# Padding the constant tiles of a two-layer decoder so that the transposed activations begin at a multiple of 64 bytes

## The chip, the cores and the metric

The kernel runs on one core of a Trainium2 chip. The time is device microseconds of that core for one execution. Before the change the median of three runs is 966.6 us (965.89 to 967.51).

## What is computed

A decoder trunk of two layers on 256 tokens of width 1024, in float32. Each layer has three sub-layers with a norm before and after: a SwiGLU (width 2816), a mixer, and a second SwiGLU. Cut to what matters:

```python
for l in range(DEPTH):                                   # DEPTH = 2
    f = swiglu(rms_norm(x, ffn1_pre_g[l]), ffn1_w_gu[l], ffn1_w_down[l])
    x = x + 0.5 * rms_norm(f, ffn1_post_g[l])
    m = hybrid_mixer(rms_norm(x, mix_pre_g[l]), mix_w_in[l], mix_w_out[l], ...)
    x = x + rms_norm(m, mix_post_g[l])
    f = swiglu(rms_norm(x, ffn2_pre_g[l]), ffn2_w_gu[l], ffn2_w_down[l])
    x = x + 0.5 * rms_norm(f, ffn2_post_g[l])

def swiglu(x, w_gu, w_down):
    g, u = jnp.split(x @ w_gu, 2, axis=-1)
    return (jax.nn.silu(g) * u) @ w_down
```

The mixer is one product into 2566 columns, three mixers side by side on groups of those columns (a gated linear recurrence, a state-space scan over two chunks of 128 tokens, and a gated causal mixing over tokens), and one product back to 1024 columns.

## The kernel before

**Numbers.** Every large product is done as three matmuls on values split into a high and a low part: high by high, high by low, low by high. The parts have the type fp32r. Small products (transposes by an identity matrix, the scan's products) are plain fp32.

**The tile nT.** `nT` holds x transposed, 128 features on the partitions, and in each partition `[2, 8, 256]` numbers: the part (high, low), the block of 128 features, and the token. It is written before each sub-layer by `pre` (four transposes into a PSUM bank, a cast for the high part, a subtraction for the low one) and read by two kinds of matmul:

- *A-steps* (line 425, `mm3` called from `a_step`): a 128-token slice of nT is the stationary operand, that is, loaded as weights; the split weights of the model move, 512 or 390 columns. They make the first block of each SwiGLU and the first two groups of the mixer.
- *B-tiles* (line 704, `b_tile`): a 128-column slice of the model's weights is stationary, and 256 tokens of nT move. They make the rest of both SwiGLUs' first products and of the mixer's.

```python
st = tuple(self.nT[:, i, k, t * P:(t + 1) * P] for i in range(2))            # a_step
self.mm3(bk[0][:, :w], st, (wt[:, 0, :w], wt[:, 1, :w]), start, stop)
...
wh, wl = (w[:, i, col:col + P] for i in range(2))                            # b_tile
xh, xl = self.nT[:, 0, k, :], self.nT[:, 1, k, :]
for i, (a, b) in enumerate(((wh, xh), (wh, xl), (wl, xh))):
    self.keep(self.nc.tensor.matmul(out, a, b, start=..., stop=...))
```

The products back to width 1024 (`down`) also go through `mm3` at line 425, but with the hidden values as the stationary operand (slots s_a or s_m) and 512 columns of weights moving. Every such matmul is preceded by one weight load (LDWEIGHTS) of 128 columns.

**Memory of a partition.** Tiles are taken in the order in which they are first asked for, each rounded up to 32 bytes. `setup` takes x0, x1, `pf` (per-feature parameters, 180 numbers, 720 bytes), nT, `ident` (the identity), `tri` (a triangle of ones), `ones` (one number), `ident_r`, `later` and `mhalf` (one number); `layer_params` takes `pb` (530 numbers), `wst`, `wbd` and more. Behind them stand small tiles, three staging buffers `stg` for the weights that come in by DMA, and the slots: `s_w` (17 split weights of 4 KB), `s_a` (13), `s_m` (8), `s_f` (3). The places in bytes of a partition, with the rest that they leave when divided by 64:

| tile | before | rest | after | rest |
|---|---|---|---|---|
| x0, x1, pf | 16512, 20608, 24704 | 0 | the same | 0 |
| nT | 25440 | 32 | 25472 | 0 |
| ident, tri | 41824, 42336 | 32 | 41856, 42368 | 0 |
| ones | 42848 | 32 | 42880 | 0 |
| ident_r, later | 42880, 43392 | 0 | 42944, 43456 | 0 |
| mhalf | 43904 | 0 | 42884 | 4 |
| pb | 43936 | 32 | 43968 | 0 |
| wst, wbd, gp | 46080, 48128, 51200 | 0 | 46144, 48192, 51264 | 0 |
| stg (first), s_a0, s_w0 | 58176, 82752, 90944 | 0 | 58240, 82816, 91008 | 0 |

All slices of nT that matmuls read begin a multiple of 512 bytes behind nT's own start, and so do the slices of the slots that the large products read, so a tile's rest holds for each of its operands there.

**Order.** The order of the work is fixed when the program is built, by a planner with costs of its own (class `Chain`, `pump`, the table `T`); those costs know nothing of addresses. Weights come through the SP queue into `stg`, ScalarE makes the high part (lines 396, 400), VectorE the low part (lines 397, 401), and TensorE uses a slot until `release`.

Of the kernel before, what the change touches and what calls it, by code (L numbers as in the profile page):

```python
# [8 lines left out]
F32 = mybir.dt.float32  # L9
# [6 lines left out]
P = 128  # L16
# [3 lines left out]
DEPTH = 2  # L20
# [84 lines left out]
NP_ = _off  # L105
BCOL = {"dtb": (0, 6), "alog": (6, 6), "dsk": (12, 6), "lng": (18, 256), "lnb": (274, 256)}
NB_ = 530


class Chain:  # L110
    """A side computation: a generator whose operations are issued when their inputs are due."""

    def __init__(self, k, t=None):
        self.k = k
# [107 lines left out]
class Kernel:  # L222
# [35 lines left out]
        self.wt, self.wh, self.wready, self.slot_time = {}, {}, {}, {}  # L258
        self.extra, self.keep_free = 0, 4

    # ---------------------------------------------------------------- memory
    def get(self, shape, dtype=F32, kind="a"):
        tag = self.free_slots[kind].pop(0)
        return self.scr.tile(shape, dtype, tag=tag, name="s_" + tag), (kind, tag)
# [24 lines left out]
        o, w = BCOL[name]  # L289
        return self.pb[:, o:o + w]  # L290

    # ---------------------------------------------------------------- issue order
    def keep(self, ins, pin=False):
        if pin or self.now() < PIN:
            self.tc.keep_in_program_order(ins)
# [39 lines left out]
    def drain(self):  # L335
        self.wait_for(lambda: not self.chains)

    # ---------------------------------------------------------------- weights
    def dma_chunk(self):
        ci = self.next_dma  # L340
        self.next_dma += 1
# [74 lines left out]
        self.slot_time[h] = self.now()  # L416
        self.put(h)

    # ---------------------------------------------------------------- main products
    def mm3(self, out, st, mv, start, stop):  # L420
        (sh, sl), (mh, ml) = st, mv
        mm = self.nc.tensor.matmul
# [11 lines left out]
        st = tuple(self.nT[:, i, k, t * P:(t + 1) * P] for i in range(2))  # L434
        self.mm3(bk[0][:, :w], st, (wt[:, 0, :w], wt[:, 1, :w]), start, stop)

    # ---------------------------------------------------------------- setup
    def setup(self):
        nc, cp = self.nc, self.cp
        self.cur = 0  # L440
        self.x = [cp.tile([P, D], F32, name=f"x{t}") for t in range(2)]
        nc.sync.dma_start(out=self.x[0], in_=self.x_d[0, 0:P, :])
        self.pf = cp.tile([P, DEPTH * NP_], F32, name="pf")
        nc.scalar.dma_start(out=self.pf, in_=self.pf_d)
        self.T["dma"] = 3.4
        self.dma_chunk()
        nc.sync.dma_start(out=self.x[1], in_=self.x_d[0, P:2 * P, :])
        self.T["dma"] += 1.46
        self.nT = cp.tile([P, 2, KT, SEQ], F32R, name="nT")
        self.ident = cp.tile([P, P], F32, name="ident")  # L450
        make_identity(nc, self.ident)
        self.tri = cp.tile([P, P], F32, name="tri")
        make_upper_triangular(nc, self.tri)
        self.ones = cp.tile([P, 1], F32, name="ones")
        nc.gpsimd.memset(self.ones, 1.0)
        self.ident_r = cp.tile([P, P], F32R, name="ident_r")
        nc.scalar.copy(self.ident_r, self.ident)
        self.later = cp.tile([P, P], F32R, name="later")
        nc.vector.tensor_scalar(out=self.later, in0=self.tri, scalar1=1.0, scalar2=1e30, op0=ALU.subtract, op1=ALU.mult)
        self.mhalf = cp.tile([P, 1], F32, name="mhalf")  # L460
        nc.gpsimd.memset(self.mhalf, -0.5)
        self.T["pool"] = 2.0

    def softplus(self, c, out, x, n, tag):
        """out = softplus(x) for [P, n] operands."""
        m, z, z2, p = (self.single([P, n], tag + s) for s in ("m", "z", "q", "p"))
        yield from c.stt(n, m, x, -1.0, x, ALU.mult, ALU.min)
        yield from c.act(n, m, m, AF.Exp, table="exp")
        yield from c.ts(n, z, m, 2.0, ALU.add)
        yield from c.op("dve", 0.15, self.nc.vector.reciprocal, z, z)  # L470
        yield from c.tt(n, z, m, z, ALU.mult)
        yield from c.tt(n, z2, z, z, ALU.mult)
        yield from c.ts(n, p, z2, 1.0 / 15, ALU.mult)
        for k in (13, 11, 9, 7, 5, 3):
            yield from c.stt(n, p, p, 1.0 / k, z2, ALU.add, ALU.mult)
        yield from c.stt(n, p, p, 1.0, z, ALU.add, ALU.mult)
        yield from c.ts(n, m, x, 0.0, ALU.max)
        yield from c.stt(n, out, p, 2.0, m, ALU.mult, ALU.add)

    def layer_params(self, l):  # L480
        nc, lp = self.nc, self.lp
        yield self.now() + 20.0
        self.pb = lp.tile([P, NB_], F32, tag="pb", name="pb")
        self.keep(nc.scalar.dma_start(out=self.pb, in_=self.pb_d[l:l + 1, :].partition_broadcast(P)), True)
        self.wst = lp.tile([P, 4, P], F32, tag="wst", name="wst")
        self.keep(nc.scalar.dma_start(out=self.wst, in_=self.wst_d[l]), True)
        raw, hr = self.get([P, 6, 64], F32, "f")
        self.keep(nc.scalar.dma_start(out=raw, in_=self.wri_d[l]), True)
        self.wbd = lp.tile([P, 6, P], F32, tag="wbd", name="wbd")
        c = Chain(self)  # L490
        c.pin = True
        yield from c.op("pool", 0.8, nc.gpsimd.memset, self.wbd, 0.0)
        c.t += 20.0
        cpy = nc.gpsimd.tensor_copy
        yield from c.op("pool", 0.8, cpy, out=self.wbd[0:64, :, 0:64], in_=raw[0:64])
        yield from c.op("pool", 0.8, cpy, out=self.wbd[64:128, :, 64:128], in_=raw[64:128])
        self.put(hr)
        yield from c.ptt(512, self.wst, self.wst, self.tri.unsqueeze(1).to_broadcast([P, 4, P]), ALU.mult)
        nl = self.single([P, 3], "nl")
        yield from c.ts(3, nl, self.pcol(l, "lam", 0, 3), -1.0, ALU.mult)  # L500
        self.cl = lp.tile([P, 2, 3], F32, tag="cl", name="cl")
        sp = self.single([P, 3], "spl")
        yield from self.softplus(c, sp, nl, 3, "sl")
        yield from c.ts(3, self.cl[:, 0, :], sp, -8.0, ALU.mult)
        yield from c.ts(3, self.cl[:, 1, :], sp, 8.0, ALU.mult)
        self.na = lp.tile([P, 6], F32, tag="na", name="na")
        yield from c.act(6, self.na, self.bcol("alog"), AF.Exp, table="exp")
        yield from c.ts(6, self.na, self.na, -1.0, ALU.mult)
        c.flag(("params", l))
# [3 lines left out]
        self.keep(self.nc.scalar.dma_start(out=t, in_=self.gp_d[i:i + 1, :].partition_broadcast(P)), True)  # L513
        return t

    # ---------------------------------------------------------------- norms
    def rstd_of(self, c, ss, n, eps, name):
        v = self.small(1, name + "v")
        if n == 2:
# [11 lines left out]
        yield from c.act(n, self.junk()[:, :n], src, AF.Square, scale=scale, accum_out=out)  # L531

    def post(self, t, banks, gp, half, nxt):
        """x[t] += (0.5 if half else 1) * rms_norm(result, gp); then the next sub-layer's operand."""
        c = Chain(self)
        ev = self.ev[t]
        ss = self.small(2, "pss")
# [1 line left out]
        for n in range(2):  # L539
            yield from c.until(("acc", self.phase_of(nxt), t, n))  # L540
            a, v = c.fork(), c.fork()
            ps, tag, _ = banks[n]
# [24 lines left out]
        return self.cur_phase  # L567

    def pre(self, t, nxt, halves):
        """The operand of the next sub-layer, x transposed and split into two parts, and 1 / rms(x) by token.  # L570

        Products take x as it is; 1 / rms(x) goes to their results. A swiglu keeps it off u, and with it off
        the whole sub-layer's result, whose own norm then adds eps / rs^2 instead of eps.
        """
        kind, _, ph = nxt
        xt = self.x[t]
        for q in range(2):
            c = halves[q]
            ps, tag = yield from c.aux()
# [8 lines left out]
        c = halves[1]  # L588
# [14 lines left out]
        ps, tag = yield from c.aux()  # L603
# [2 lines left out]
        c.free_aux(tag)  # L606
        c.flag(("rb", ph, t))

    # ---------------------------------------------------------------- ffn
    def evac_block(self, b, g, u, gtag, utag, t, width, hT, ph):  # L610
        c = Chain(self)
        sil, h1 = yield from c.get([P, 512], F32, "m")
# [77 lines left out]
        return self.down(lhs, d, gp, True, nxt)  # L690

    def b_tile(self, bk, half, d, col, last):
        """One 128-column tile of the product, features by tokens."""
        self.T["pe"] = max(self.T["pe"], bk[2] + HOP)
        for t in range(2):
            for q in range(2):
                self.need(("nT", self.phase, t, q))
        out = bk[0][:, half * SEQ:(half + 1) * SEQ]
        for k in range(KT):
            w = self.unit(d + k)  # L700
            wh, wl = (w[:, i, col:col + P] for i in range(2))
            xh, xl = self.nT[:, 0, k, :], self.nT[:, 1, k, :]
            for i, (a, b) in enumerate(((wh, xh), (wh, xl), (wl, xh))):
                self.keep(self.nc.tensor.matmul(out, a, b, start=k == 0 and i == 0, stop=k == KT - 1 and i == 2))  # L704
                self.T["pe"] += SEQ * 0.000417
                self.pump()
            if last:
                self.release(d + k)
# [63 lines left out]
            self.put(*lhs[i][3])  # L772
        return d + 2 * n_k

    # ---------------------------------------------------------------- mixer
    def mixer(self, l, d, nxt):
        nc, ph = self.nc, self.phase
        gp = self.load_gpost(l * 3 + 1)
# [184 lines left out]
            c.flag(("mixT", ph, f, t))  # L963

    def decay(self, l):
        """dt, the decays within a chunk, exp(a_cs[l] - a_cs[s]) for s <= l, and the decays to its ends."""
        nc, M, ph = self.nc, self.M, self.phase
        c = Chain(self)
        d12 = lambda a: a.rearrange("p c h -> p (c h)")
        dt, ad, nacs = (self.single([P, 2, 6], n) for n in ("dt", "ad", "nacs"))  # L970
# [90 lines left out]
        self.put(h_xdt, h_xd, M["zs_h"], M["bc_h"])  # L1061

    def scores(self, c, ch, bT, cT):
        """E[s, l] * (c[l] . b[s]) for s <= l, each head."""
        M, ph = self.M, self.phase
        e = M["E"][ch][0]
        ps, tag = yield from c.aux()
# [46 lines left out]
            yield from self.split_out(c, 3 + f, ch, ps[:, f * P:(f + 1) * P])  # L1114
        c.free_aux(tag)

    # ---------------------------------------------------------------- program
    def build(self):
        self.rs, self.ev = [None, None], [None, None]
        self.setup()  # L1120
# [78 lines left out]
```

## Time and profile before

| what | value |
|---|---|
| median of three runs | 966.6 us |
| profiled execution, first to last instruction | 963.5 us (3.1 us below the median; what lies outside the span is not in the trace) |
| granted TensorE clock | 0.998 of full speed |
| TensorE matmul (PE) | busy 98% of the span |
| weight loads (PEld) | 90%, beside the matmuls |
| VectorE, ScalarE, GpSimd | 67%, 60%, 4% |
| DMA | 182 GB/s in the mean |

A matmul's own duration in the trace is longer than the distance to the next one, since matmuls are pipelined: a 128x256 B-tile matmul is shown as 279 ns long, while they start about 117 ns apart. What one costs is therefore read from the distance between starts: the start of a run of equal matmuls, the start of what follows it, and the count.

### The profile page before, as it was taken

Reading aid. Unit: us, or ns where it says so; the run is one execution under the profiler, and the core shown is the slowest. Engines: PE = TensorE matmul, PEld = TensorE weight load, DVE = VectorE, ACT = ScalarE, POOL = GpSimd, SP = SyncE. Lnnn points to the kernel's source line nnn. Section 1 sums busy time; section 2 is a strip of 40 time slices with the busy share of each in tenths; the row PEclk is TensorE's granted clock in tenths of the full one; section 3 lists DMA queues with packets and bytes.
Section 4 is the critical chain, followed back from the end, with each engine's and each line's share of the span. In section 5 each row is a group of like instructions: output and inputs, shape, how many; then the busy total and the mean of one; then the engine's idle time right before and its main releaser. Section 6 shows DMA issues by size and latency. Waiting matters only on the chain.

```text
span 963.5 us, 16052 instructions
## 1 busy us (share of the span) xinstructions
PE 945.1 (98%) x6292; PEld 862.9 (90%) x6292; DVE 649.1 (67%) x1169; ACT 580.4 (60%) x1057; POOL 40.1 (4%) x58
## 2 busy tenths in 40 slices
PE   7999999999999999999999999999999999999997
PEld 6999998889986999998889999888999779999885
DVE  5876666566899856676565666666588996566632
ACT  7865555576967765555564555555589685454531
POOL 1100000001001100000010000000010110000000
PEclk9999999999999999999999999999999999999999
DMA  8855555443246945566435555663431566455621
GB/s 309 290 202 205 188 208 208 154 168 116 88 136 212 327 165 175 176 218 221 172 130 198 175 183 209 221 224 113 177 127 45 206 231 236 137 193 210 214 80 44
DMA packets 26717, 175.66 MB, mean 182 GB/s; under 512 B 2960, under 2 KB 3344, under 8 KB 7824
## 3 DMA queue, kind: packets, MB, share of 16 engines
q1 hardware_dynamic: 24768, 169.93, 50.0%
q10 hardware_dynamic: 1872, 4.70, 1.4%
q8 instruction: 49, 0.80, 0.3%
q14 instruction: 28, 0.23, 0.1%
HBM read 173.57 MB, written 1.05 MB: 181 GB/s over the span
## 4 chain that ended last, share of the span: by engine, by line
PE 89%; DVE 6%; ACT 2%; POOL 1%; issue 1%; DMA 0%; DVEq 0%; POOLq 0%; ACTq 0%
PE acc L704 46%; PE acc L425 39%; PE acc L137 4%; DVE s_w L401 2%; DVE s_a L137 1%; ACT s_a L137 1%; DVE x L137 1%; DVE s_f L137 1%; POOL postr L137 1%; DVE nT L137 1%; ACT L137 1%; POOL rs L137 0%; DMA x<-in_x_dram 0%; ACT junk L137 0%; POOL lnr L137 0%
## 5 line engine op out<-in xcount | busy, mean ns | idle before, releaser
L704 PE MATMUL acc<-nT,s_w 128*128 128x256 f32 x3900 | 467.5, 279 | 0.0
L704 PEld LDWEIGHTS acc<-nT,s_w 128*128 128x128 f32 x3900 | 460.3, 188 | 0.7
L401 DVE SCALAR_TENSOR_TENSOR s_w<-stg,pf,s_w 128x512 fp32r<-128x512 f32 (+2 forms) x435 | 299.2, 735 | 112.8 <-ACT s_w L400 112.5
L400 ACT ACTIVATE s_w<-stg,pf 128x512 fp32r<-128x512 f32 (+2 forms) x435 | 279.4, 701 | 113.7 <-PE acc L704 62.1
L425 PE MATMUL acc<-s_w,s_a 128*128 128x512 f32 x984 | 227.4, 390 | 0.0
L425 PEld LDWEIGHTS acc<-s_w,s_a 128*128 128x128 f32 x984 | 184.1, 188 | 37.9
L397 DVE TENSOR_TENSOR s_w<-stg,s_w 128x512 fp32r<-128x512 f32 x184 | 121.9, 687 | 61.9 <-ACT s_w L396 61.7
L396 ACT CAST s_w<-stg 128x512 fp32r<-128x512 f32 x184 | 107.0, 619 | 68.6 <-PE acc L425 36.7
L425 PE MATMUL acc<-s_w,nT 128*128 128x512 f32 (+1 forms) x522 | 129.3, 394 | 1.2 <-DVE nT L137 1.0
L425 PEld LDWEIGHTS acc<-s_w,nT 128*128 128x128 f32 x522 | 95.7, 189 | 21.6 <-DVE nT L137 2.3
L137 ACT ACTIVATE s_m<-s_m 128x512 f32<-128x512 f32 x36 | 22.6, 632 | 79.9 <-DVE s_m L137 79.9
L137 DVE TENSOR_TENSOR s_m<-acc,s_m 128x512 f32<-128x512 f32 (+1 forms) x64 | 35.7, 562 | 31.3 <-PE acc L704 25.8
L425 PE MATMUL acc<-s_w,s_m 128*128 128x512 f32 x192 | 48.0, 399 | 0.0
L425 PEld LDWEIGHTS acc<-s_w,s_m 128*128 128x128 f32 x192 | 34.8, 188 | 7.0 <-ACT s_m L137 0.5
L137 POOL TENSOR_TENSOR postr<-postv,mhalf 128x1 f32<-128x1 f32 x12 | 10.7, 893 | 705.7 <-DVE postv L137 705.7
L137 ACT CAST s_a<-s_m 128x512 fp32r<-128x512 f32 x36 | 22.1, 615 | 27.4 <-DVE s_m L137 26.9
L137 DVE TENSOR_TENSOR s_f<-acc,gp 128x512 f32<-128x512 f32 x24 | 16.5, 687 | 32.9 <-ACT junk L137 32.9
L137 ACT ACTIVATE junk<-acc 128x512 bf16<-128x512 f32 x24 | 14.2, 594 | 38.7 <-PE acc L425 38.2
L137 DVE TENSOR_TENSOR s_m<-acc,rb 128x512 f32<-128x512 f32 x36 | 24.7, 687 | 14.4 <-PE acc L704 14.4
L137 DVE TENSOR_TENSOR s_a<-s_m,s_a 128x512 fp32r<-128x512 f32 x36 | 24.7, 687 | 10.0 <-ACT s_a L137 10.0
L137 DVE SCALAR_TENSOR_TENSOR s_a<-s_f,pf,s_a 128x255 f32<-128x255 f32 (+2 forms) x60 | 28.5, 496 | 3.9 <-ACT s_a L137 3.9
L704 PE MATMUL acc<-nT,s_a 128*128 128x256 f32 x180 | 26.8, 279 | 0.0
(130 smaller groups left out, 526.0 us busy)
## 6 DMA issues: line engine op xcount, KB each, us to landing
stg<-in_wts_dram SPq DMA_DIRECT2D x147, 1024.0 KB, 5.0
stg<-in_wts_dram SPq DMA_DIRECT2D x12, 768.0 KB, 4.3
stg<-in_wts_dram SPq DMA_DIRECT2D x4, 780.0 KB, 4.4
gp<-in_gpost_dram ACTq DMA_DIRECT2D x6, 512.0 KB, 5.7
x<-in_x_dram SPq DMA_DIRECT2D x2, 512.0 KB, 4.4
out_dram<-x SPq DMA_DIRECT2D x4, 256.0 KB, 2.0
pb<-in_pb_dram ACTq DMA_DIRECT2D x2, 265.0 KB, 5.2
stg<-in_wts_dram SPq DMA_DIRECT2D x2, 256.0 KB, 4.6
```

The lines of the kernel that those rows point to most:

```text
L137: ins = fn(*args, **kw)
L396: self.keep(nc.scalar.copy(hi, src))
L397: self.keep(nc.vector.tensor_tensor(out=lo, in0=src, in1=hi.bitcast(F32), op=ALU.subtract))
L400: self.keep(nc.scalar.activation(hi, src, AF.Copy, scale=s))
L401: self.keep(nc.vector.scalar_tensor_tensor(out=lo, in0=src, scalar=s, in1=hi.bitcast(F32), op0=ALU.mult, op1=ALU.subtract))
L425: self.keep(mm(out, a, b, start=start and i == 0, stop=stop and i == 2))
L704: self.keep(self.nc.tensor.matmul(out, a, b, start=k == 0 and i == 0, stop=k == KT - 1 and i == 2))
```

## The change

Three allocations are rounded up, and two one-number tiles share one. pf takes 192 numbers instead of 180, so nT behind it begins 32 bytes later; pb takes 544 instead of 530; `ones` and `mhalf` become columns 0 and 1 of a tile `cols` of 16 numbers. The tiles that stood 32 bytes past a multiple of 64 (nT, ident, tri, ones, pb) stand on one; the staging buffers and slots, which stood on one already, move by 64 bytes. The instructions, their order on each engine and their semaphores are those of before; only addresses differ, and the row pitch of pf and pb. (The diff's other lines take away comments and docstrings.)

```diff
-        self.pf = cp.tile([P, DEPTH * NP_], F32, name="pf")
-        nc.scalar.dma_start(out=self.pf, in_=self.pf_d)
+        self.pf = cp.tile([P, 192], F32, name="pf")
+        nc.scalar.dma_start(out=self.pf[:, :DEPTH * NP_], in_=self.pf_d)
...
-        self.ones = cp.tile([P, 1], F32, name="ones")
+        cols = cp.tile([P, 16], F32, name="cols")
+        self.ones, self.mhalf = cols[:, 0:1], cols[:, 1:2]
         nc.gpsimd.memset(self.ones, 1.0)
...
-        self.mhalf = cp.tile([P, 1], F32, name="mhalf")
         nc.gpsimd.memset(self.mhalf, -0.5)
...
-        self.pb = lp.tile([P, NB_], F32, tag="pb", name="pb")
+        self.pb = lp.tile([P, 544], F32, tag="pb", name="pb")[:, :NB_]
```

## The prediction

> **What bounds the kernel.** The table above has TensorE busy for 98% of the span. I read next the chain of work that ended last, by engine.
>
> ```profile
> PE 89%; DVE 6%; ACT 2%; POOL 1%; issue 1%; DMA 0%; DVEq 0%; POOLq 0%; ACTq 0%
> ```
>
> TensorE carries 89% of the chain. So the pace of its matmuls sets the time, and the question is whether the pace depends on where an operand begins. The groups by shape tell which matmuls read nT ("acc<-nT,s_w" is a B-tile with nT moving; "acc<-s_w,nT" an A-step with nT stationary):
>
> ```profile
> L704 PE MATMUL acc<-nT,s_w 128*128 128x256 f32 x3900 | 467.5, 279 | 0.0
> L704 PE MATMUL acc<-nT,s_a 128*128 128x256 f32 x180 | 26.8, 279 | 0.0
> L425 PE MATMUL acc<-s_w,s_a 128*128 128x512 f32 x984 | 227.4, 390 | 0.0
> L425 PE MATMUL acc<-s_w,nT 128*128 128x512 f32 x438 | 112.9, 403 | 1.2 <-DVE nT L137 1.0
> L425 PE MATMUL acc<-s_a,nT 128*128 128x512 f32 x42 | 12.1, 395 | 0.0
> L425 PE MATMUL acc<-s_w,nT 128*128 128x390 f32 x84 | 17.4, 346 | 0.0
> L425 PE MATMUL acc<-s_a,nT 128*128 128x390 f32 x12 | 2.8, 340 | 0.0
> ```
>
> 4080 B-tile matmuls and 576 A-steps read nT; the products back (s_a stationary) do not, and there both operands already begin on a multiple of 64 bytes. They are the comparison that this trace offers. Pace is the distance between starts; these rows of the time line (start, length, matmuls, count) hold one undisturbed run each and the start of what follows it:
>
> ```profile
> 609.04 45.09 PE L425 MATMUL acc<-s_w,s_a 128*128 128x512 f32 x198
> 653.97 1.52 PE L425 MATMUL acc<-s_a,s_a 128*128 128x512 f32 x6
> ...
> 504.99 2.96 PE L425 MATMUL acc<-s_w,nT 128*128 128x512 f32 x12
> 507.79 2.04 PE L704 MATMUL acc<-nT,s_w 128*128 128x256 f32 x16
> ...
> 196.99 2.83 PE L425 MATMUL acc<-s_w,nT 128*128 128x390 f32 x15
> 199.66 0.60 PE L137 MATMUL acc<-ident,x 128*128 128x128 f32 x4
> ```
>
> - Both operands on 64, 512 columns: (653.97 - 609.04) / 198 = 226.9 ns, 0.443 ns a column.
> - nT stationary, 512 columns: (507.79 - 504.99) / 12 = 233.3 ns, 0.456 ns a column.
> - nT stationary, 390 columns: (199.66 - 196.99) / 15 = 178.0 ns, 0.456 ns a column.
>
> For B-tiles the chain has the long runs, here with all the pieces of B-tiles that lie on it in the four SwiGLUs (start, length, line, count):
>
> ```profile
> 32.98 3.27 PE acc L704 x28
> 37.27 97.43 PE acc L704 x835
> 321.05 2.69 PE acc L704 x23
> 324.29 98.12 PE acc L704 x841
> 507.95 1.87 PE acc L704 x16
> 510.26 98.94 PE acc L704 x848
> 795.60 2.22 PE acc L704 x19
> 798.26 98.59 PE acc L704 x845
> ```
>
> 98.59 / 845 = 116.7 ns for 256 columns: again 0.456 ns a column. That is the reading on which I rest. The three shapes in which one operand begins 32 bytes past a multiple of 64 cost the same per column, whether that operand is stationary or moving and whether 256, 390 or 512 columns move; the one shape with both operands on a multiple costs 0.443. The excess grows with the columns, so it is no fixed cost of a weight load, and it looks like a price of the two operands not being in step. After the change all of them are in step.
>
> **The sum.** B-tiles: 116.7 against 226.9 / 2 = 113.5 ns, 3.2 ns less each. The rows above hold 28 + 835 + 23 + 841 + 16 + 848 + 19 + 845 = 3455 of them, with nothing between that waits, so 3455 x 3.2 = 11.1 us. In the mixer only part of them lies on the chain:
>
> ```profile
> 217.14 7.47 PE acc L704 x64
> 224.95 1.40 PE acc L704 x11
> 227.23 3.42 ACT s_a L137 x12
> ...
> 242.38 1.29 PE acc L704 x11
> 246.49 8.65 PE acc L704 x74
> 261.20 1.29 PE acc L704 x11
> 263.71 1.64 PE acc L704 x14
> ```
>
> From 227.23 the chain goes through ScalarE and VectorE (the state-space decays) to 242, and the B-tiles of that stretch run in its shade: a gain there only lengthens TensorE's wait. On the chain are 64 + 11 + 11 + 74 + 11 + 14 = 185 a layer, 370 x 3.2 = 1.2 us.
>
> A-steps gain 233.3 - 226.9 = 6.4 ns at 512 columns, and 390 x 0.0126 = 4.9 ns at 390. The chain holds these:
>
> ```profile
> 17.35 15.64 PE acc L425 x67
> 307.56 4.66 PE acc L425 x20
> 312.66 8.39 PE acc L425 x36
> ```
>
> 67 in the first SwiGLU (a few more ahead of it, amid waits for the first weights), 20 + 36 in the second of layer 0 and as many in that of layer 1 (the other 40 of 96 go while VectorE still splits weights, and gain nothing); all 96 of layer 1's first; 48 of 512 and 48 of 390 columns in each mixer. That is 67 + 56 + 56 + 96 + 96 = 371 x 6.4 = 2.4 us and 96 x 4.9 = 0.5 us.
>
> Sum 11.1 + 1.2 + 2.4 + 0.5 = 15.2 us off the span of 963.5, which leaves 948.3. The median of the runs is 3.1 us above that span, so 966.6 - 15.2 = 951.4 us.
>
> **What costs nothing, and its cover.** No instruction, wait or queue entry is added or moved. The split of the weights must keep up with a faster TensorE:
>
> ```profile
> 325.00:420.00 95.00, 95.00 (x816) 95.00 (x816) 61.54 (x109) 54.68 (x87) 0.00 (x0) 1.00 0.55 193
> 620.00:660.00 40.00, 40.00 (x178) 33.14 (x177) 22.18 (x34) 20.34 (x33) 0.00 (x0) 1.00 0.61 212
> ```
>
> (Window; then its length, and busy us of PE, PEld, DVE, ACT, POOL; clock; DMA share; GB/s.) In the B-tiles of a SwiGLU VectorE is busy 61.5 of 95 us, ScalarE 54.7, DMA 0.55; 3% more pace asks 3% more of them. The clock is 1.00 in both windows, so the difference between 0.456 and 0.443 is not the clock. The tail behind the last matmul stays.
>
> The fp32 products with ident or tri move from 32 to 0 as well:
>
> ```profile
> L137 PE MATMUL acc<-ident,x 128*128 128x128 f32 x96 | 16.5, 302 | 7.7 <-DMA x<-in_x_dram 4.7 <-DVE x L137 2.9
> L137 PE MATMUL acc<-tri,ad 128*128 128x128 f32 x48 | 6.6, 274 | 0.0
> L137 DVE TENSOR_TENSOR nT<-acc,nT 128x512 fp32r<-128x512 f32 x24 | 15.9, 684 | 0.0
> L137 DVE TENSOR_TENSOR s_a<-s_m,s_a 128x512 fp32r<-128x512 f32 x36 | 24.7, 687 | 10.0 <-ACT s_a L137 10.0
> ```
>
> With the 92 other products by ident (of s_a, rs and s_m) that is under 240 matmuls; at the 3% above, 3 ns each either way, plus or minus 0.7 us at most. I take 0: they are another mode, and no pair of rows compares them. VectorE's writes into nT (684 ns) are no slower than the same operation on a slot (687 ns), so 0 there too. The two parameter loads (pf, pb) land off the chain, and a GpSimd operand 4 bytes past 64 is one number a partition: 0.
>
> **Rivals.**
>
> *Only the A-steps gain.* A B-tile needs one load of 128 weights per 256 columns, and the window at 325 shows PEld busy for all of its 95.00 us, against 33.14 of 40 in the product back. If the load sets the B-tile's 116.7 ns, its stationary operand (s_w) was on 64 before, and nothing changes. Then 966.6 - 2.9 = 963.7 us. Against it: the 0.456 would have to equal that of the A-steps by chance.
>
> *Nothing changes.* nT may be slow for a reason other than the 32 bytes: it lies low in the partition, among the constants, far from the slots. Then 966.6 us. For it: no other fp32r tile of that region is read in a long run, so region and 32 bytes are not told apart. [...]
>
> *More than the step.* Out of step may cost B-tiles more, since there both reads go on all the time. A floor from this trace is the pace of short fp32 products with a weight load each:
>
> ```profile
> 237.39 1.00 PE L137 MATMUL acc<-s_a,wst 128*128 128x64 f32 x8
> 238.20 1.42 PE L704 MATMUL acc<-nT,s_w 128*128 128x256 f32 x10
> ```
>
> 0.81 / 8 = 101 ns; down to there would be 15.7 x 3825 = 60 us, 904 us. It is a far end: 64 columns move there, in another mode. Half-way to it, 108 ns, gives 966.6 - 33 - 2.9 = 931 us.
>
> *Slower.* With both operands at the same rest, both reads of a B-tile could want the same part of memory at each step; the products back don't show it, because their weight load ends early. Priced as one such step upwards (3.2 ns x 3825 = 12.2 us, less the A-steps' 2.9): 976 us. It decides the sign as soon as a B-tile loses more than 2.9 / 3825 = 0.8 ns. For it: PEld's full window. Against it: s_a and s_w are at the same rest in the products back, and that is the fastest pace per column here.
>
> **How the numbers follow.** Forecast 0.61, only the A-steps 0.10, nothing 0.13, more than the step 0.08, slower 0.08. The forecast's own range is 947 (every nT matmul gains in full: 4080 x 3.2 + 480 x 6.4 + 96 x 4.9 = 16.6 us, and fp32 products a little) to 956 (a third of it lost to new waits). The range that is to hold 8 in 10 goes on down to 944, towards the larger gain, and up to 967, which takes in "only the A-steps" and "nothing". About 0.2%, 1.9 us, is what the runs here can tell from no change. Faster 0.79 (forecast, A-steps, more), same 0.13, slower 0.08.
>
> **What would show it.** In the changed kernel the B-tile runs on the chain should read about 113.5 ns (845 in 95.9 us instead of 98.6), the A-steps 226.9 and 173 ns, the products back an unchanged 226.9; the four long runs of B-tiles each about 2.7 us shorter, and TensorE's waits in the mixer a little longer. I am wrong if B-tiles stay at 116.7 with A-steps at 226.9 (the load bounds them), if neither moves (it was never the 32 bytes), or if new waits for s_w stand in the long runs.

## The result and the profile after

The changed kernel takes 977.2 us (median of four runs, 976.1 to 977.9) against 966.4 us before (four runs): ratio 1.0104, interval 1.009 to 1.0118. It is slower by 10.8 us, where I forecast 15.2 us less. The profiled execution spans 974.3 us against 963.5, so the whole difference lies inside the span.

The chain of waits of the changed kernel, with the four long runs of B-tiles (start, length, line, count), which answer to those of the prediction:

```profile
37.24 100.19 PE acc L704 x835
...
326.97 100.92 PE acc L704 x841
...
515.36 101.76 PE acc L704 x848
...
806.25 101.40 PE acc L704 x845
```

Each is longer: by 2.76, 2.80, 2.82 and 2.81 us, together 11.2. A B-tile matmul takes 101.40 / 845 = 120.0 ns where it took 116.7. Between the runs the time hardly changed: from the end of the first to the start of the second it is 189.54 us (before 189.59), from the second to the third 87.47 (before 87.85).

The time line of the changed kernel, for the A-steps (start, length, matmuls, count, and the start of what follows):

```profile
27.63 4.92 PE L425 MATMUL acc<-s_w,nT 128*128 128x512 f32 x21
32.39 3.51 PE L704 MATMUL acc<-nT,s_w 128*128 128x256 f32 x28
...
199.71 2.83 PE L425 MATMUL acc<-s_w,nT 128*128 128x390 f32 x15
202.38 0.60 PE L137 MATMUL acc<-ident,x 128*128 128x128 f32 x4
```

At 512 columns an A-step now takes 4.76 / 21 = 226.7 ns, as forecast (233.3 before). At 390 columns it takes 2.67 / 15 = 178.0 ns, just as before. The other engines have nearly the work that they had. This is the prediction's window, taken of the changed kernel (it now opens 2 us ahead of the long run, and GpSimd's three instructions begin in those 2 us):

```profile
325.00:420.00 95.00, 95.00 (x794) 94.97 (x793) 63.31 (x110) 56.30 (x89) 2.81 (x3) 1.00 0.55 191
```

TensorE is still busy in all of it at a clock of 1.00, and no wait has come in; it does 794 matmuls where it did 816.

### The profile page after: what moved, and what is told of

The parts are those of the page before. It is cut to its first block, busy times and chain, and to the rows that moved or that the text cites. A ratio compares the mean times of both kernels' runs of the same rounds, so it can differ in the third digit from the quotient of the medians.

```text
span 974.3 us, 16052 instructions
## 1 busy us (share of the span) xinstructions
PE 956.2 (98%) x6292; PEld 875.9 (90%) x6292; DVE 648.7 (67%) x1169; ACT 580.4 (60%) x1057; POOL 39.7 (4%) x58
## 4 chain that ended last, share of the span: by engine, by line
PE 91%; DVE 6%; POOL 1%; issue 1%; ACT 0%; DMA 0%; DVEq 0%; POOLq 0%; ACTq 0%
PE acc L704 48%; PE acc L425 38%; PE acc L137 4%; DVE s_w L401 2%; DVE x L137 1%; DVE s_a L137 1%; DVE s_f L137 1%; POOL postr L137 1%; DVE nT L137 1%; POOL rs L137 0%; DMA x<-in_x_dram 0%; ACT junk L137 0%; POOL lnr L137 0%; DVE bst L137 0%; DVE s_m L137 0%
## 5 line engine op out<-in xcount | busy, mean ns | idle before, releaser
L704 PE MATMUL acc<-nT,s_w 128*128 128x256 f32 x3900 | 480.2, 283 | 0.0
L704 PEld LDWEIGHTS acc<-nT,s_w 128*128 128x128 f32 x3900 | 473.0, 192 | 0.6
L425 PE MATMUL acc<-s_w,nT 128*128 128x512 f32 (+1 forms) x522 | 127.2, 390 | 1.5 <-DVE nT L137 1.2
L137 POOL TENSOR_TENSOR postr<-postv,cols 128x1 f32<-128x1 f32 x12 | 10.7, 893 | 715.1 <-DVE postv L137 715.1
```

The source lines that it names most:

```text
L137: ins = fn(*args, **kw)
L425: self.keep(mm(out, a, b, start=start and i == 0, stop=stop and i == 2))
```

## The experiments

All kernels but the two probes issue the instructions of before, in the same order on each engine and with the same waits; only addresses differ. "Distance" is the start of nT less the start of the slots, modulo 256 (a period that the first probe suggests and no run proves). Before it was 32, after the change 0. In a B-tile this is the moving operand's start less the stationary one's, and the probes count it so; in an A-step, where nT is the stationary operand, the sign is the other.

**nT alone put back.** The change with nT at 32 past a multiple of 64 again, everything else as changed.

```diff
-        self.pf = cp.tile([P, 192], F32, name="pf")
+        self.pf = cp.tile([P, 184], F32, name="pf")
...
         self.nT = cp.tile([P, 2, KT, SEQ], F32R, name="nT")
+        cp.tile([P, 8], F32, name="pad")
```

> The changed kernel with nT alone put back to 32 bytes past a multiple of 64 (pf 184 numbers instead of 192, 32 bytes of padding behind nT); identity, triangle, pb, the shared column tile and all slots stay where the change put them. Theory 1 (the distance of nT from the slots, modulo 64, sets the pace): as before the change, 966 us, B-tiles 116.7 ns, A-steps of 512 columns 233.3 ns. Rival (one of the other moved tiles, or the slots' move by 64, made it slower): 977 us, B-tiles 120.0 ns.

It took 972.1 us, ratio to before 1.006 (1.0045 to 1.0075): neither of the two. The longest runs on its chain:

```profile
326.66 99.52 PE acc L705 x841
...
803.62 100.00 PE acc L705 x845
```

100.00 / 845 = 118.3 ns. nT accounts for the difference to the changed kernel, since it alone moved; but 32 past a multiple of 64 is not what made 116.7. The slots moved by 64 with the change, so the distance is now -32 and not +32. Theory 1 was wrong in the period, or in taking both signs for one.

**The slots moved instead.** The kernel before, with the slots 32 bytes further and nT where it was.

```diff
+        self.scr.tile([P, 8], F32, tag="pad", name="pad")
         self.x = [cp.tile([P, D], F32, name=f"x{t}") for t in range(2)]
```

> The kernel before, with all slots (s_a, s_w, s_m, s_f) moved by 32 bytes through padding ahead of them; nT stays at 25440, 32 past a multiple of 64. So both operands of a B-tile have the same rest again, but it is 32 and not 0. Theory 1 (the distance sets the pace): as after the change, 977 us, B-tiles 120.0 ns, A-steps of 512 columns 226.7 ns. Rival (nT's own place sets it, by its rest or by its region of the partition): as before the change, 966 us, B-tiles 116.7 ns. The products back, whose operands move together, stay at 226.7 ns by both.

It took 976.5 us, ratio 1.0109 (1.0092 to 1.0125), which is the changed kernel's time, although nT never moved:

```profile
17.08 15.22 PE acc L425 x67
...
806.07 101.40 PE acc L705 x845
```

101.40 / 845 = 120.0 ns again, and the A-steps of the first row take 15.22 / 67 = 227.2 ns, against 15.64 / 67 = 233.4 before. So nT's own place, its region and its rest modulo 64 are not the cause. Distance 0 is, whether both operands stand on 64 or both at 32 past it.

**A map of distances.** A probe of bare matmuls, which leaves out the whole computation: 72 matmuls a row, the moving tile m_ and the stationary tile s_ shifted by the bytes that their names say.

> A probe that computes nothing of the reference (it copies x out): runs of 72 fp32r matmuls, each with its own weight load, of 256, 512 and 390 moving columns, with the moving operand (tiles m_...) or the stationary one (s_...) a named number of bytes past a multiple of 512. Theory 1 (the distance of the two operands, modulo 64): moving at 32 with stationary at 0 gives 116.7 ns at 256 columns and 233.3 at 512; 0 with 0 and 32 with 32 give 120.0 and 226.7; 64, 128 and 256 are as 0, 96 as 32; other distances lie on 120.0, 116.7 or another step, and show whether there is one that is better than both. Rival (each operand's own place): 32 with 32 differs from 0 with 0. Rival (a larger period than 64, or other addresses): 64, 96, 128 or 256 differ from 0 and 32.

Its time line; the pace of a row is the distance to the next row's start over 72:

```profile
41.06 8.32 PE L51 MATMUL acc<-m_sixteen,s_zero 128*128 128x256 f32 x72
49.22 8.80 PE L51 MATMUL acc<-m_twentyfour,s_zero 128*128 128x256 f32 x72
57.86 8.56 PE L51 MATMUL acc<-m_thirtytwo,s_zero 128*128 128x256 f32 x72
66.26 8.80 PE L51 MATMUL acc<-m_forty,s_zero 128*128 128x256 f32 x72
...
92.06 8.64 PE L51 MATMUL acc<-m_sixtyfour,s_zero 128*128 128x256 f32 x72
100.54 8.80 PE L51 MATMUL acc<-m_ninetysix,s_zero 128*128 128x256 f32 x72
109.18 8.70 PE L51 MATMUL acc<-m_onetwentyeight,s_zero 128*128 128x256 f32 x72
117.72 8.79 PE L51 MATMUL acc<-m_twofiftysix,s_zero 128*128 128x256 f32 x72
126.35 8.48 PE L51 MATMUL acc<-m_zero,s_eight 128*128 128x256 f32 x72
...
143.20 8.68 PE L51 MATMUL acc<-m_zero,s_thirtytwo 128*128 128x256 f32 x72
151.72 8.64 PE L51 MATMUL acc<-m_zero,s_fortyeight 128*128 128x256 f32 x72
160.19 8.33 PE L51 MATMUL acc<-m_zero,s_sixtyfour 128*128 128x256 f32 x72
168.36 8.80 PE L51 MATMUL acc<-m_thirtytwo,s_thirtytwo 128*128 128x256 f32 x72
176.99 8.56 PE L51 MATMUL acc<-m_sixteen,s_sixteen 128*128 128x256 f32 x72
185.39 16.50 PE L51 MATMUL acc<-m_zero,s_zero 128*128 128x512 f32 x72
...
583.43 12.65 PE L51 MATMUL acc<-m_thirtytwo,s_zero 128*128 128x390 f32 x72
595.92 13.11 PE L51 MATMUL acc<-m_forty,s_zero 128*128 128x390 f32 x72
```

At 256 columns: distance 16 gives 113.3 ns, 32 gives 116.7 (the kernel before), 256 gives 119.9 as 0 does in the kernels, -32 gives 118.3 (the kernel with nT put back), -64 gives 113.5, 64 gives 117.8, 96 gives 120.0. So +64 and 0 differ, and so do 96 and 32: the period is not 64. A period of 256 fits at this one pair. Both at 32 give 119.9, but both at 16 give 116.7, so the distance is not the whole of it; whether the tiles' own places count there, or a second pattern of the kind found below, this row does not tell. At 390 columns a distance of 32 gives (595.92 - 583.43) / 72 = 173.5 ns, where the A-steps of the kernel before, at -32, had 178.0: the sign counts. Where a kernel and the probe share a distance (0, 32, -32) their paces agree, and two distances, 16 and -64, promise better than 116.7.

**Distance 16 and distance -64 in the kernel.** The first moves nT by 16 bytes, the second puts 64 bytes between nT and the slots, so that everything stays on a multiple of 64.

Distance 16:

```diff
+        nt = cp.tile([P, 2 * KT * SEQ + 8], F32R, name="nT")
+        self.nT = nt[:, 4:4 + 2 * KT * SEQ].rearrange("p (i k s) -> p i k s", i=2, k=KT)
...
-        cols = cp.tile([P, 16], F32, name="cols")
+        cols = cp.tile([P, 8], F32, name="cols")
```

Distance -64:

```diff
         self.nT = cp.tile([P, 2, KT, SEQ], F32R, name="nT")
+        cp.tile([P, 16], F32, name="pad")
```

> The changed kernel with nT 16 bytes further (25488), so that it stands 16 past the slots' rest of 256; the slots stay, identity and triangle are back at 32 past a multiple of 64. Theory 2 (the two reads of a B-tile, the moving operand and the next weight load, get in each other's way in a pattern that their distance modulo 256 sets, as the probe's runs show): B-tiles 113.3 ns as the probe has for moving 16 ahead, A-steps of 512 columns 233.3 and of 390 columns 180.0; 966.4 - 3825 x 3.3 = 953.7 us. Rival (whole multiples of 64, or the absolute place, decide, and the probe's pace does not carry over): B-tiles 116.7 ns or more, 966 us or more.

> The changed kernel with 64 bytes of padding behind nT: nT stays at 25472, all slots and constants behind it stand 64 further, everything on multiples of 64 as after the change. Distance of nT from the slots -64 modulo 256. Theory 2 (distance modulo 256): B-tiles 113.3 ns (the probe's moving at 0 with stationary at 64), A-steps of 512 columns 228.9 ns and of 390 columns 176.7 (its moving at 64 with stationary at 0); 966.4 - 12.7 - 375 x 4.4 = 952.0 us. Rival (the rest modulo 64 decides, which is as after the change): B-tiles 120.0 ns, 977 us.

Distance 16 took 968.6 us over ten runs that spread from 963.9 to 971.9; ratio 1.0011 (0.9991 to 1.003), no difference. Distance -64 took 954.9 us, ratio 0.9879 (0.9847 to 0.9912). Two long runs of each, first of distance 16, then of -64:

```profile
325.06 98.13 PE acc L705 x841
510.92 100.63 PE acc L705 x848
```

```profile
321.15 95.33 PE acc L705 x841
504.06 99.88 PE acc L705 x848
```

Distance 16 has 98.13 / 841 = 116.7 and 100.63 / 848 = 118.7 ns, where the probe had 113.3. Distance -64 has 113.4 and 117.8. One program, one distance, and two paces, each the mean over more than 800 matmuls. The other long runs repeat them: at distance 16 97.42 / 835 = 116.7 and 100.28 / 845 = 118.7 ns, at -64 94.65 / 835 and 95.80 / 845, both 113.4. Two runs at 116.7 and two at 118.7 in one execution speak for paces of their own rather than means of a changing mixture; I take it from this that a run of matmuls falls into one of several patterns. That can widen the spread of the times, and one row of a probe may show only one of the patterns. The rival by which only multiples of 64 count is out: at -64 all tiles stand on 64 as in the changed kernel, and it is 22 us faster.

**A second probe**, in steps of 16, upwards and downwards, and with one operand reduced to a single column.

> A second probe that computes nothing of the reference: the pace of 256 columns with the moving operand (n_...) 0 to 240 bytes past the stationary one (slot) in steps of 16, in rising and then in falling order of the distances; of 512 and 390 columns with n_... stationary and slot moving; and runs in which one of the operands is a single column read again and again (one), so that it sweeps no memory. Theory 2 (the moving read and the weight load's read meet in memory): with either operand a single column the excess over the columns' own time vanishes, about 109 ns at 256 columns and 215 at 512 (the probe's 113.3 and 226.7 are its lowest with two sweeps); the two orders give the same pace at each distance. Rival (a fixed cost of the weight load or of the matmul, not a meeting in memory): the single-column runs keep 113 to 120 and 227 to 233 ns. Rival (the state that a run starts from decides, not the distance): the two orders differ.

```profile
17.54 8.71 PE L53 MATMUL acc<-n_sixteen,slot 128*128 128x256 f32 x72
26.09 8.56 PE L53 MATMUL acc<-n_thirtytwo,slot 128*128 128x256 f32 x72
...
43.01 8.32 PE L53 MATMUL acc<-n_sixtyfour,slot 128*128 128x256 f32 x72
51.16 8.79 PE L53 MATMUL acc<-n_eighty,slot 128*128 128x256 f32 x72
...
68.44 8.32 PE L53 MATMUL acc<-n_oneonetwo,slot 128*128 128x256 f32 x72
76.59 8.70 PE L53 MATMUL acc<-n_onetwoeight,slot 128*128 128x256 f32 x72
...
685.17 8.39 PE L53 MATMUL acc<-n_oneonetwo,slot 128*128 128x256 f32 x72
693.41 8.80 PE L53 MATMUL acc<-n_ninetysix,slot 128*128 128x256 f32 x72
...
710.69 8.64 PE L53 MATMUL acc<-n_sixtyfour,slot 128*128 128x256 f32 x72
719.17 8.68 PE L53 MATMUL acc<-n_fortyeight,slot 128*128 128x256 f32 x72
...
736.17 8.57 PE L53 MATMUL acc<-n_sixteen,slot 128*128 128x256 f32 x72
744.58 8.80 PE L53 MATMUL acc<-n_zero,slot 128*128 128x256 f32 x72
753.21 8.33 PE L53 MATMUL acc<-n_zero,one 128*128 128x256 f32 x72
761.38 8.22 PE L53 MATMUL acc<-one,n_zero 128*128 128x256 f32 x72
769.44 8.23 PE L53 MATMUL acc<-one 128*128 128x256 f32 x72
777.50 16.64 PE L53 MATMUL acc<-n_zero,one 128*128 128x512 f32 x72
793.98 15.90 PE L53 MATMUL acc<-one,n_zero 128*128 128x512 f32 x72
809.72 15.91 PE L53 MATMUL acc<-one 128*128 128x512 f32 x72
```

Distance 64 had 113.2 ns on the way up and 117.8 on the way down: two patterns at one distance, so the distance alone does not fix the pace. Distance 16 had 118.8 and 116.8, which are the two paces of the kernel at 16; the first probe's 113.3 came in neither order. Distance 192, which is -64 modulo 256, had 117.8 and 113.8 (rows at 110.71 and 642.77 us), near the two paces of the kernel at -64. Of the fifteen distances above 0, six (16, 32, 64, 112, 160 and 192) differ between the orders by 1 ns or more. Distance 112 had 113.2 and 114.4, where the expectation for the kernel at 112 says 113.3 for both orders. The period of 256 stays open: 240 and 208, which would be -16 and -48, had 117.2 and 119.2 in both orders, against 118.5 and 117.6 in the first probe.

With a moving operand of one column ("one,n_zero") 256 columns take 111.9 and 512 take 218.6 ns, a little over the expected 109 and 215, which were an estimate with no run behind it. The two measured paces give (218.6 - 111.9) / 256 = 0.417 ns a column, and 5.2 ns for each matmul. So the excess over that, 1 to 11 ns at 256 columns and 8 to 19 at 512 over both probes (the most at distance 4 of the first: 123.1 and 237.4 ns), comes with a moving operand that sweeps memory. With a stationary operand of one column the excess stays, 113.5 and 228.9 ns, so theory 2 as I had put it, that two sweeps meet, is not borne out: one sweep and a weight load from a fixed place are enough. How the distance acts on the pace no run here shows, nor what a sweep without weight loads would cost, since every matmul had its own.

**Distance 112 in the kernel**, and -64 once more for its spread. Against the changed kernel, the one-number tiles move into pf's padding and, in softplus, four small tiles become one, to make the distance fit.

```diff
-        self.pf = cp.tile([P, 192], F32, name="pf")
+        self.pf = cp.tile([P, 184], F32, name="pf")
...
+        nt = cp.tile([P, 2 * KT * SEQ + 8], F32R, name="nT")
+        self.nT = nt[:, 4:4 + 2 * KT * SEQ].rearrange("p (i k s) -> p i k s", i=2, k=KT)
...
-        cols = cp.tile([P, 16], F32, name="cols")
-        self.ones, self.mhalf = cols[:, 0:1], cols[:, 1:2]
+        self.ones, self.mhalf = self.pf[:, 180:181], self.pf[:, 181:182]
...
+        if n == 3:
+            one = self.single([P, 16], tag)
+            m, z, z2, p = (one[:, 4 * i:4 * i + 3] for i in range(4))
...
```

> The changed kernel with nT 112 bytes past the slots' rest of 256 (nT data at 25456, slots at 0 modulo 256; to make room the two one-number tiles stand in pf's padding and four small tiles of layer_params share one; instructions, order and waits unchanged). 112 is the distance at which the second probe had 113.3 ns for 256 columns in both orders. Theory 2 (distance modulo 256, with more than one steady state at some distances): B-tiles 113.3 ns in all four SwiGLUs, A-steps 233.3 (512) and 180.0 (390); 966.4 - 12.7 + 0.2 = 953.9 us, with runs closer together than those of the -64 kernel. Rival (which state a run locks into is chance at every distance but 0): some long runs at 117 ns or more, runs spread over 954 to 966 us.

> The -64 kernel once more, for its spread: it had 953.4 to 958.9 us in four runs, and its profiled run had one of four SwiGLUs at 117.8 ns a B-tile instead of 113.3. Theory 2 with two steady states: each SwiGLU at 117.8 costs 864 x 4.4 ns = 3.8 us, so runs lie at about 952.5 us plus a multiple of 3 to 4. Rival (the spread is noise of the chip): times without such steps, and profiles with every SwiGLU at 113.3.

Distance 112 took 954.8 us (954.0 to 956.1), ratio 0.9879 (0.9865 to 0.9894), where 953.9 was expected. Its four long runs:

```profile
37.45 94.65 PE acc L708 x835
...
321.59 95.33 PE acc L708 x841
...
504.82 96.18 PE acc L708 x848
...
789.77 95.80 PE acc L708 x845
```

All four are at 113.4 ns. Distance -64 took 954.2 us, ratio 0.9878 (0.9861 to 0.9894); four of its five runs lie at 954.0 to 954.4 and one at 957.0, one step higher, and its first four were 953.4, 953.4, 956.4 and 958.9. Theory 2 asks for steps of 3.8 us; these are 3.0 and 5.5. Only the profiled runs show which SwiGLU was in which pattern, and they show a second cause of spread: in the second profile the third long run takes 96.14 us where it took 99.88, but 1.5 us of it are lost again ahead of the first long run, which starts at 38.83 us instead of 37.32 (the chain there goes through ScalarE and VectorE from 26.37 to 37.53 us, where in the first profile it stays on TensorE), so that the time is 2.0 us less (954.4 against 956.4). For the other runs the patterns are inferred, and other noise is not excluded. Both kernels beat the one before by 12 us, and the changed one by 22.

## Why the prediction was wrong

- **What bounds the kernel** was right: TensorE's pace set the time. The change added 10.8 us and distance -64 took 22 off again, with the same instructions at other addresses.
- **The step that failed** is the reading on which I said that I rest: three shapes with one operand at 32 cost 0.456 ns a column, the shape with both on 64 costs 0.443, hence "a price of the two operands not being in step" that holds for each shape. The three equal figures were a coincidence of one distance: at distance 0 the same three shapes cost 120.0 / 256 = 0.469, 178.0 / 390 = 0.456 and 226.7 / 512 = 0.443 ns a column. They also mixed two signs, since the moving operand stood 32 bytes ahead of the stationary one in B-tiles and 32 behind it in A-steps; with the sign of the B-tiles 390 columns take 173.5 ns, 0.445 a column. So the excess at 256, 390 and 512 columns goes its own way with the distance: 0 is the best seen at 512 columns with both operands sweeping (226.7) and among the worst at 256 (120.0). I carried a comparison at 512 columns over to 256, where the trace of before had one distance only and so nothing to compare.
- **The B-tile term** was -12.3 us; the long runs alone gave +11.2. **The A-steps of 512 columns** came out as priced, 226.7 ns. **Those of 390** gained nothing (178.0 before and after), another sign that the per-column rule was none.
- **The forecast 113.5 ns** is a pace that exists: the kernels at -64 and 112 run at 113.4 (one of the eight long runs at -64 apart) and take 954 to 955 us, near the 951.4 of the sum. But a multiple of 64 has no part in it. The changed kernel stands on one and runs at 120.0, and at 112 nT stands 48 past one.
- **The rival "slower"** said 976 us: 3.2 ns more a B-tile, measured 3.3, and 977.2 us. It had 0.08. Its argument, that the product back does not show what happens when both reads go on all the time, is the one that should have had the weight: the window with PEld busy 95.00 of 95.00 us was the hint that B-tiles may be another regime. That its number came so near is in part luck: the step upwards had been given the size of the supposed step downwards, and its mechanism, both operands at the same rest, is not the cause, since at -64 they have the same rest modulo 64 and run at 113.4.
- **"Only the A-steps gain"** and **"more than the step"** are out: the B-tiles did change, and no kernel or probe with a sweeping moving operand came below 113.2 ns, against the 108 of the second.
- **"Nothing changes"**, the rival that nT's region sets the pace, is out by the kernel with moved slots. A move of the slots by 32 bytes, with nT where it was, takes the time from 966.4 to 976.5 us.
- **The covers** held: ScalarE, VectorE and DMA kept up both at 120.0 and at 113.4 ns, and the fp32 products with ident made no difference that shows: with ident at 32 (the kernel with moved slots) and at 0 (the changed one) the time is 976.5 and 977.2 us.

## What to carry to other kernels

In this kernel, where TensorE is the bound and every matmul has its own weight load, the place of the moving tile relative to the stationary one was worth about 1% either way (977.2 us at distance 0 and 954.8 at 112, against 966.4 at 32); roundness of an address was no guide to it. In such a kernel, map the pace over distances with bare matmuls of the kernel's own width, in more than one order, then confirm in the kernel, since some distances had more than one pace (64 in the second probe: 113.2 and 117.8 ns). Compare paces only at the same number of moving columns and the same sign of the distance: 0 was among the worst at 256 columns (120.0 ns) and the best at 512 (226.7), and in the first probe 390 columns took 173.5 ns at 32 and 177.8 at -32.

## What the runs showed of the hardware

- The pace of fp32r matmuls of 256 columns, each with its weight load, lay between 113.2 and 123.1 ns by addresses and pattern alone (granted clock 1.00; left out is the first row of each probe, which holds TensorE's first matmuls and comes to 149.6 and 146.5 ns), that of 512 columns between 226.7 and 237.4 ns; with a moving operand that sweeps no memory it is 111.9 and 218.6.
- One distance had more than one pace, each as the mean of a run of more than 800 matmuls: at -64 in one execution 113.4 (three runs) and 117.8 ns (one), at 16 in one execution 116.7 and 118.7 (two each). At 0 every long run was at 120.0 (two kernels, four long runs each).
- Still open: how the distance acts on the pace, whether the period is 256, why both tiles at 16 differ from both at 0 (116.7 against 120.0), and what chooses the pattern of a run.
